# A float32 decoder trunk on one core: who subtracts the high parts of the weights

## The chip, the cores and the metric

The kernel runs on one core of a Trainium2 chip. The metric is the time of one execution on the device in microseconds (us), as the median of several runs. A profile is one execution that the hardware profiler recorded; its span runs from the first to the last instruction. The engines are named as in the profile: PE is TensorE (matrix products; PEld its loading of the stationary operand), DVE is VectorE, ACT is ScalarE, POOL is GpSimd and SP is SyncE, which issues the loads.

## The reference

Four layers act on 256 tokens of width 1024. Each layer is half an FFN, a token mixer, half an FFN, and each of the three is followed by a residual sum and a layer norm. The mixers are, by layer, DSA, FoX, MLA and DSA.

```python
for i in range(DEPTH):
    x = layer_norm(ALPHA * x + 0.5 * swiglu(x, ffn1_w13[i], ffn1_w2[i]), ln_g[i, 0], ln_b[i, 0])
    kind, j = i % N_MIXERS, i // N_MIXERS
    if kind == 0:
        y = dsa_mixer(x, dsa_w_in[j], w_out[i], cos_p, sin_p)
    elif kind == 1:
        y = fox_mixer(x, fox_w_in[j], fox_b_f[j], w_out[i])
    else:
        y = mla_mixer(x, mla_w_dqkv[j], mla_q_norm_g[j], mla_w_uq[j], mla_kv_norm_g[j],
                      mla_w_ukv[j], w_out[i], cos_m, sin_m)
    x = layer_norm(ALPHA * x + y, ln_g[i, 1], ln_b[i, 1])
    x = layer_norm(ALPHA * x + 0.5 * swiglu(x, ffn2_w13[i], ffn2_w2[i]), ln_g[i, 2], ln_b[i, 2])
```

A mixer projects x to queries, keys and values of 16 heads, forms the causal scores, the softmax and its product with the values, and multiplies by `w_out`. DSA first scores the keys with a small indexer and keeps the best of them for each query, FoX adds a bias from cumulated forget gates, and MLA projects through two low-rank latents.

## The kernel before

Each float32 product is made of three passes on TensorE. An operand is split into a high part (the value rounded to 12 significant bits) and a low part (the value less its high part), and a product is high by high plus high by low plus low by high, accumulated in PSUM (`mm3`, `mm3b`).

All weights stream through SBUF once. `unit` (line 127) takes up to 1024 columns: a load into one of six `raw` buffers, a cast to the high part on ScalarE (L144) and a subtraction for the low part (L145), both into one of 15 slots that weights and larger activations share. Two settings act on it. `self.share`, where it is not 0, cuts a unit into two pieces (`PIECES`), each with its own cast and subtraction, and gives every third unit's two subtractions to GpSimd; the other units' go to VectorE. Where it is 0, a unit is one piece and VectorE has it. `run` sets it to 3 ahead of every FFN and every mixer, and `ffn` sets it to 0 ahead of its main loop. So it acts in the mixers and, in seven of the eight FFNs, on the eight units of the first four FFN tiles (`gate` and `up`).

An FFN goes over its tiles in pairs: products of gate and up, silu, products with the second matrix. The norm at its end (`layer_norm`) adds the products to x (L232), takes the mean (L241), squares on ScalarE (L242), forms the reciprocal root on GpSimd (L218), and scales (L245, L247). Then TensorE transposes x (L202), and ScalarE and VectorE split the result into `xh` and `xl` (L190, L191 in `split`). Two token tiles of 128 follow one another through this.

In a mixer, `heads` goes over eight pairs of heads. A pair's scores are added to their bias with a row maximum (L393), the maximum is turned into a bias (L397 or L400 and L401), ScalarE takes the exponent (L403), VectorE the reciprocal (L404) and four scalings (L406). `turn` transposes the weights (L416 to L418) and splits them (`pth`, `ptl`), and `weigh` multiplies by the values. Between these steps stand products of later projections and of `w_out`, by a table that says how many. GpSimd also does the small touches of slots (L78), the zeros of the block-diagonal keys (L497, L498), the ropes (L372 to L375) and FoX's masks (L705, L706).

The order on each engine is made by the tile framework's scheduler from the order of the code and its own idea of durations. It is fixed when the program is built, and each engine executes its own in order.

Of the kernel before, what the change touches and what calls it, by code (L numbers as in the profile page):

```python
"""Hybrid decoder trunk (DSA / FoX / MLA token mixers between half-step SwiGLU FFNs) on one core.

Matrix products are float32 products on the tensor engine's one-pass float32r path: an operand is
split exactly into hi = round12(v) and lo = v - hi (12 significant bits each), and a product takes the
three passes hi*hi + hi*lo + lo*hi, accumulated in float32 in PSUM. Weights stream through SBUF once,
in units of up to 2048 columns; activations stay on chip.
"""
# [9 lines left out]
F32 = mybir.dt.float32  # L17
# [26 lines left out]
SHARE_F, SHARE_M = 3, 3  # L44
PIECES, PBUFS = 2, 1
# [6 lines left out]
class Net:  # L52
    def __init__(self, ctx, tc, a):
        self.tc, self.nc, self.a = tc, tc.nc, a
        pool = lambda name, bufs, **k: ctx.enter_context(tc.tile_pool(name=name, bufs=bufs, **k))
        self.cp = pool("const", 1)
        self.sp = pool("state", 1)
        self.kp = pool("work", 1)
        self.pp = pool("psum", 4, space=bass.MemoryType.PSUM)
        self.n = 0  # L60
        self.late, self.subs, self.share = [], 0, 0
        self.consts()

# [8 lines left out]
    def slot(self, *dims, p=P, dt=F32R, touch=True):  # L72
        """One of the 8 KB slots that weights and the larger activations share, viewed as [p, *dims].
        Slots are given in order of their first write: a touch takes one ahead of its data."""
        n = int(np.prod(dims))
        z = self.t(self.kp, [P, 2048], dt, "slot", SLOTS)[:p, :n]
        if touch:
            self.nc.gpsimd.memset(z[:, :1] if dt == F32 else z[:, :1].bitcast(F32), 0.0)  # L78
        names = "abcde"[:len(dims)]
        return z.rearrange(f"p ({' '.join(names)}) -> p {' '.join(names)}", **dict(zip(names, dims)))  # L80
# [11 lines left out]
    def consts(self):  # L92
        """What the first products need; the rest comes in late_consts."""
        nc, a = self.nc, self.a
        self.mhalf = self.const("mhalf", [P, 1])
        nc.vector.memset(self.mhalf, -0.5)
        self.ident = self.const("ident", [P, P])
        nc.sync.dma_start(self.ident, a["c_ident"])
        self.x = [self.t(self.sp, [P, D], F32, f"x{t}", 1) for t in range(NT)]
        self.load_x(0)  # L100
        # the activation table and the tensor engine's clock are brought up while the loads run
        z = self.tok()
        nc.gpsimd.memset(z, 0.0)
        nc.scalar.activation(z[:, :1], z[:, :1], AF.Silu)
        ps = self.ps("b")
        for i in range(WARM):
            nc.tensor.matmul(ps[:, :P], z[:, P:2 * P], z[:, 2 * P:3 * P], start=True, stop=True)
# [19 lines left out]
    def unit(self, src):  # L127
        """Loads and splits a DRAM view [128, a, b], up to 1024 columns at a time; gives (hi, lo) [128, b]
        of each of a."""
        nc = self.nc  # L130
        _, a, b = src.shape
        out = []
        step = -(-a // -(-a // (1024 // b)))
        for i in range(0, a, step):
            n = min(step, a - i)
            raw = self.w([P, 1024], "raw", RAWS)[:, :n * b]
            z = self.slot(2, n * b, touch=False)
            h, l = z[:, 0], z[:, 1]
            nc.sync.dma_start(raw.rearrange("p (a b) -> p a b", a=n), src[:, i:i + n])
            self.subs += 1  # L140
            e = nc.gpsimd if self.share and self.subs % self.share == 0 else nc.vector
            m = n * b // (PIECES if self.share else 1)
            for c in [slice(o, o + m) for o in range(0, n * b, m)]:
                nc.scalar.copy(h[:, c], raw[:, c])  # L144
                e.tensor_sub(l[:, c], raw[:, c], h[:, c].bitcast(F32))  # L145
            out += [(h[:, j * b:(j + 1) * b], l[:, j * b:(j + 1) * b]) for j in range(n)]
        return out

    def rows(self, w, k0, k1, c0, c1):
        """Rows k0*128.. of a [K, N] matrix as [128, k, cols]."""  # L150
        return w[k0 * P:k1 * P, c0:c1].rearrange("(k p) c -> p k c", p=P)

    def cols(self, w, c0, n):
        """Columns c0..c0+n of a [1024, N] matrix: (hi, lo) of each K tile."""
        return self.unit(self.rows(w, 0, KT, c0, c0 + n))
# [13 lines left out]
    def flush(self):  # L169
        """Emits the transposes of x that wait for a place among other products."""  # L170
        for z in self.late:
            z()
        self.late = []

    def proj(self, us, t, out, flush=None):
        """out[tokens of tile t, n] = x @ w over the K tiles of us."""
        q = slice(t * P, (t + 1) * P)
        for k, (h, l) in enumerate(us):
            if k == flush:
                self.flush()  # L180
            self.mm3(out, self.xh[:, k, q], self.xl[:, k, q], h, l, k == 0, k == len(us) - 1)

    def projb(self, us, i, out, k0=0):
        """out[columns i*128.. of w, tokens] = (x @ w) transposed; us are the K tiles from k0."""
# [36 lines left out]
    def layer_norm(self, t, acc, mult, eps, last=False):  # L221
        """x <- LN(mult * x + acc); scaling the argument by two and eps by four changes nothing."""
        nc = self.nc
# [30 lines left out]
    def begin_out(self, w, n, src, tag):  # L254
        """A [256 n, 1024] matrix by units of two K tiles; src(i) gives (hi, lo) [128, tokens] of K tile i."""
        self.ow, self.on, self.osrc = w, n, src
        self.ou, self.acc, self.otag = {}, {}, tag

    def out_mm(self, k, t, halves=(0, 1)):
        """Adds unit k's product for token tile t."""  # L260
# [13 lines left out]
    def out_end(self, t, ks):  # L274
        """The last units of a token tile, the first half of the columns done early."""
# [7 lines left out]
    def ffn(self, w13, w2, ln, first=False, last=False):  # L283
# [4 lines left out]
        if not first:  # L288
            # the first four ff tiles by token tile, tokens on partitions
# [25 lines left out]
        self.share = 0  # L315
        for j in range(pairs):
# [5 lines left out]
            # a bank to each column tile where the K tiles come in two parts  # L322
# [43 lines left out]
    def rope(self, z, tab, t, half):  # L366
        """Turns z [128, heads, 2*half] in place; tab [128, tile, (cos cos | sin sin), 2*half]."""
# [9 lines left out]
    def softmax(self, scores, bias, scale, cq=None):  # L377
        """One pair of heads: scores(t) gives PSUM [128 queries, 2, keys]. The products are emitted; the rest is
        left as a function that gives the weights by t and head."""
# [3 lines left out]
        def rest():  # L383
# [14 lines left out]
            else:  # L398
                # the row's own cum enters the logits and the maximum alike
# [11 lines left out]
    def turn(self, views):  # L411
        """The weights of a pair transposed: [128 keys, (head, query)] of key tile 0 and 1."""
# [12 lines left out]
    def weigh(self, ph, pl, v, i, oh, ol):  # L425
        """O transposed of a pair; columns i*128.. of v are its values, oh and ol [128, tokens]."""
# [12 lines left out]
    def heads(self, project, weights, w_out, plan, done=0, begun={}, more=()):  # L439
        """The eight pairs of heads, two to a group. project(g) yields between chunks of its work and then  # L440
        has group g ready; weights(p) gives the softmax of pair p and (v, column block) of its values.
        Between the steps of a pair stand chunks of later groups' projections (plan: how many after a pair's
        softmax and after its transposes) and products of w_out."""
# [41 lines left out]
    def values(self, w, c0, v):  # L485
        """V of two pairs from columns c0.. of w."""
# [7 lines left out]
    def new_kz(self, n=2):  # L494
        """Block diagonal K of pairs: a head's rows are zero in the other head's columns."""
# [10 lines left out]
    def pair_scores(self, qh, ql, kh, kl):  # L506
        """qh, ql [128 (2 heads), 256 tokens]; kh, kl [128, 2, 256] block diagonal."""
# [10 lines left out]
    def dsa(self, w_in, w_out, ln):  # L518
# [51 lines left out]
        def select(t):  # L570
            """Additive mask of the keys that are causal and among the top ones."""
# [60 lines left out]
    def fox(self, w_in, b_f, w_out, ln):  # L632
        nc = self.nc
        scale = HD ** -0.5
        # forget gates: heads on partitions
# [22 lines left out]
        # log sigmoid(z) = min(z, 0) - log(1 + exp(-|z|))  # L658
# [6 lines left out]
        # every query's row of key terms, by a broadcast through memory  # L665
# [32 lines left out]
        def weights(p):  # L698
            g, i = p // 2, p % 2
            q, kz, ck = ready[g]  # L700
            # mask the diagonal blocks of this pair's key terms
# [131 lines left out]
    def run(self):  # L833
# [4 lines left out]
        for i in range(DEPTH):  # L838
            j = i // 3
            self.share = SHARE_F  # L840
            self.ffn(a["ffn1_w13"][i], a["ffn1_w2"][i], (i, 0), first=i == 0)
            self.share = SHARE_M
# [7 lines left out]
            self.share = SHARE_F  # L850
# [13 lines left out]
def _shape_constants():  # L864
    """Identity, causal mask and rotary tables: they depend on the shapes alone."""
# [34 lines left out]
```

## Time and profile before

| what | value |
|---|---|
| median of 3 runs | 2077.57 us (2077.02 to 2078.26) |
| span of the profiled execution | 2077.2 us |
| PE busy | 2021.1 us (97%) |
| DVE busy | 1271.0 us (61%) |
| ACT busy | 1030.3 us (50%) |
| POOL busy | 320.7 us (15%) |
| chain that ended last | PE 82%, DVE 12%, ACT 3% |

The profiled execution is known by its span alone; the median of the runs is 0.4 us above it. A busy share is a mean over stages: the FFNs take most of the span and the four mixers lie between them, at 197 to 352 us (DSA), 729 to 862 (FoX), 1239 to 1351 (MLA) and 1726 to 1878 (DSA). In rows of the timeline the number in brackets at the end is the idle time of the engine before the row and what ended it.

### The profile page before, as it was taken

The numbers are of one execution on the slowest core, as the hardware profiler recorded it, in microseconds if no ns is written. First come the engines' busy times: TensorE is split into PE (matmuls) and PEld (weight loads), VectorE is DVE, ScalarE is ACT, GpSimd is POOL, SyncE is SP. The second block draws the span as 40 slices with busy tenths as digits, with TensorE's granted clock in tenths as the row PEclk, the third lists the DMA queues.
The fourth block names the chain that finished last, engine by engine and source line by source line (L and its number), as shares of the span: only waits on it lengthen the run. The fifth ranks groups of instructions, "written<-read, shape, count | busy, mean of one in ns | idle before, by whom it ended". The sixth has DMA issues, their size and how long they took to land.

```text
span 2077.2 us, 34193 instructions
## 1 busy us (share of the span) xinstructions
PE 2021.1 (97%) x13430; PEld 1853.2 (89%) x13430; DVE 1271.0 (61%) x2069; ACT 1030.3 (50%) x1714; POOL 320.7 (15%) x454
## 2 busy tenths in 40 slices
PE   9999998999999998999999999899999999989998
PEld 8999986999899987799989998689989999978997
DVE  6455889544644469855465456964465546887453
ACT  5443476444444357644444436754444444675441
POOL 0002542000100145200110014400020005430000
PEclk9999999999999999999999999999999999999999
DMA  9754534665656454565665543566656564347550
GB/s 304 226 184 138 153 122 155 214 188 176 212 183 188 150 162 155 185 208 184 183 203 182 186 121 105 180 214 185 187 178 208 187 180 131 119 125 237 189 184 21
DMA packets 253025, 362.98 MB, mean 175 GB/s; under 512 B 11856, under 2 KB 204128, under 8 KB 252864
## 3 DMA queue, kind: packets, MB, share of 16 engines
q1 hardware_dynamic: 252080, 358.30, 54.7%
q0 software_dynamic: 784, 2.51, 0.4%
q8 instruction: 105, 1.72, 0.3%
q14 instruction: 56, 0.46, 0.1%
HBM read 359.69 MB, written 1.06 MB: 174 GB/s over the span
## 4 chain that ended last, share of the span: by engine, by line
PE 82%; DVE 12%; ACT 3%; issue 2%; POOL 0%; DMA 0%; SPq 0%; DVEq 0%; ACTq 0%; POOLq 0%
PE psa L166 14%; PE psa L167 14%; PE psa L165 14%; PE psb L159 8%; PE psb L160 8%; PE psb L161 8%; PE psa L159 5%; PE psa L161 5%; PE psa L160 5%; DVE slot L145 3%; DVE slot L191 2%; DVE s L406 2%; ACT s L403 1%; PE psb L202 1%; ACT slot L144 1%
## 5 line engine op out<-in xcount | busy, mean ns | idle before, releaser
L145 DVE TENSOR_TENSOR slot<-raw,slot 128x1024 fp32r<-128x1024 f32 (+4 forms) x724 | 773.1, 1089 | 617.5 <-ACT slot L144 614.9
L144 ACT CAST slot<-raw 128x1024 fp32r<-128x1024 f32 (+5 forms) x854 | 693.8, 849 | 652.0 <-issue 354.9
L166 PE MATMUL psa<-xh,slot 128*128 128x256 f32 x2496 | 707.6, 284 | 3.8 <-DVE slot L145 3.8
L165 PE MATMUL psa<-xh,slot 128*128 128x256 f32 x2496 | 707.4, 284 | 0.0
L167 PE MATMUL psa<-xl,slot 128*128 128x256 f32 x2496 | 707.1, 283 | 0.0
L166 PEld LDWEIGHTS psa<-xh,slot 128*128 128x128 f32 x2496 | 479.7, 192 | 7.6 <-DVE slot L145 4.6
L165 PEld LDWEIGHTS psa<-xh,slot 128*128 128x128 f32 x2496 | 479.6, 192 | 3.0
L167 PEld LDWEIGHTS psa<-xl,slot 128*128 128x128 f32 x2496 | 479.6, 192 | 0.0
L159 PE MATMUL psb<-slot,slot 128*128 128x512 f32 (+2 forms) x800 | 308.1, 385 | 9.0 <-DVE slot L191 4.8
L160 PE MATMUL psb<-slot,slot 128*128 128x512 f32 (+2 forms) x800 | 306.9, 384 | 1.9 <-DVE slot L191 1.9
L161 PE MATMUL psb<-slot,slot 128*128 128x512 f32 (+2 forms) x800 | 305.3, 382 | 1.2 <-DVE slot L191 1.2
L159 PE MATMUL psa<-slot,xh 128*128 128x256 f32 (+5 forms) x736 | 241.1, 328 | 0.0
L160 PE MATMUL psa<-slot,xh 128*128 128x256 f32 (+5 forms) x736 | 238.6, 324 | 0.0
L161 PE MATMUL psa<-slot,xl 128*128 128x256 f32 (+5 forms) x736 | 238.1, 324 | 0.0
L145 POOL TENSOR_TENSOR slot<-raw,slot 128x512 fp32r<-128x512 f32 (+4 forms) x130 | 183.5, 1428 | 306.1 <-ACT slot L144 297.1
L159 PEld LDWEIGHTS psb<-slot,slot 128*128 128x128 f32 (+1 forms) x800 | 150.9, 189 | 37.7 <-ACT slot L190 5.3
L78 POOL MEMSET slot<- 128x1 f32 (+1 forms) x88 | 8.5, 101 | 1118.4 <-PE psb L161 972.1
L161 PEld LDWEIGHTS psb<-slot,slot 128*128 128x128 f32 (+1 forms) x800 | 150.9, 189 | 30.9 <-DVE slot L191 1.5
L160 PEld LDWEIGHTS psb<-slot,slot 128*128 128x128 f32 (+1 forms) x800 | 151.2, 189 | 28.3 <-DVE slot L191 2.7
L159 PEld LDWEIGHTS psa<-slot,xh 128*128 128x128 f32 x736 | 140.6, 191 | 10.3 <-ACT xh L190 0.3
L160 PEld LDWEIGHTS psa<-slot,xh 128*128 128x128 f32 x736 | 140.6, 191 | 10.2
L161 PEld LDWEIGHTS psa<-slot,xl 128*128 128x128 f32 x736 | 140.4, 191 | 10.4
(150 smaller groups left out, 1696.7 us busy)
## 6 DMA issues: line engine op xcount, KB each, us to landing
raw<-in_ffn_w SPq DMA_DIRECT2D x528, 512.0 KB, 4.2
raw<-in_dsa_w_in SPq DMA_DIRECT2D x48, 512.0 KB, 3.8
raw<-in_w_out SPq DMA_DIRECT2D x32, 512.0 KB, 3.6
raw<-in_fox_w_in SPq DMA_DIRECT2D x24, 512.0 KB, 3.8
ln_g<-in_ln_g SPq DMA_DIRECT2D x12, 512.0 KB, 5.5
ln_b<-in_ln_b SPq DMA_DIRECT2D x12, 512.0 KB, 5.8
slot<-scratch_cum POOLq DMA_DIRECT2D x4, 512.0 KB, 5.4
raw<-in_mla_w_ukv SPq DMA_DIRECT2D x4, 512.0 KB, 3.9
```

Source lines behind the costliest of these rows:

```text
L144: nc.scalar.copy(h[:, c], raw[:, c])
L145: e.tensor_sub(l[:, c], raw[:, c], h[:, c].bitcast(F32))
L159: mm(out, sh, mh, start=start, stop=False)
L160: mm(out, sh, ml, start=False, stop=False)
L161: mm(out, sl, mh, start=False, stop=stop)
L165: mm(out, sh, mh, start=start, stop=False)
L166: mm(out, sl, mh, start=False, stop=False)
L167: mm(out, sh, ml, start=False, stop=stop)
L191: self.nc.vector.tensor_sub(lo, src, hi.bitcast(F32))
L202: self.nc.tensor.transpose(ps[:, i * P:(i + 1) * P], self.x[t][:, k * P:(k + 1) * P], self.ident)
L403: nc.scalar.activation(sv, sv, AF.Exp, bias=nb[:, c:c + 1], scale=scale, accum_out=l[:, c:c + 1])
L406: nc.vector.tensor_scalar(sv, sv, l[:, c:c + 1], None, op0=ALU.mult)
```

## The change

`self.share` and its count are gone; `self.pieces` says into how many pieces a unit is cut, and VectorE has all subtractions. `run` sets it to 2 ahead of an FFN, `ffn` to 1 ahead of its main loop, and nothing sets it ahead of a mixer. So the eight first units of an FFN are still cut in two, and a mixer's units are one piece each.

```diff
-SHARE_F, SHARE_M = 3, 3
...
-        self.late, self.subs, self.share = [], 0, 0
+        self.late, self.pieces = [], 1
...
-            self.subs += 1
-            e = nc.gpsimd if self.share and self.subs % self.share == 0 else nc.vector
-            m = n * b // (PIECES if self.share else 1)
+            m = n * b // self.pieces
             for c in [slice(o, o + m) for o in range(0, n * b, m)]:
                 nc.scalar.copy(h[:, c], raw[:, c])
-                e.tensor_sub(l[:, c], raw[:, c], h[:, c].bitcast(F32))
+                nc.vector.tensor_sub(l[:, c], raw[:, c], h[:, c].bitcast(F32))
...
         pairs = (NFF - f0) // 2
-        self.share = 0
+        self.pieces = 1
...
-            self.share = SHARE_F
+            self.pieces = PIECES
             self.ffn(a["ffn1_w13"][i], a["ffn1_w2"][i], (i, 0), first=i == 0)
-            self.share = SHARE_M
...
-            self.share = SHARE_F
+            self.pieces = PIECES
             self.ffn(a["ffn2_w13"][i], a["ffn2_w2"][i], (i, 2), last=i == DEPTH - 1)
```

Of the subtractions of weights, the program before has 472 of 1024 columns, 210 of 512 and 42 of other widths on VectorE and 118 of 512 and 12 of other widths on GpSimd. The changed program has 580 of 1024, 112 of 512 and 27 of other widths (384 to 960) on VectorE. The scheduler's order changes with it. The changed program's line numbers are 1 to 4 lower than those above (L142 is L145, L188 is L191, L199 is L202, L229 is L232, L242 is L245, L244 is L247, L394 is L397, L403 is L406). In names of buffers the last number is a running one; the first says which buffer.

First place: VectorE where the first FFN ends and the first DSA begins. `x0_1_71` and `x1_2_72` are x of token tiles 0 and 1, `psb_53` and `psb_54` the two halves of tile 1's last products. Before:

```order
L245 SCALAR_TENSOR_TENSOR x0_1_71<-x0_1_71,lnst_191_1842,ln_g_97_979 128x512 x2
L247 SCALAR_TENSOR_TENSOR x0_1_71<-x0_1_71,rstd_196_1852,ln_b_98_980 128x512 x2
L232 SCALAR_TENSOR_TENSOR x1_2_72,lnst_199_1908<-x1_2_72,psb_53_526 128x512
L191 TENSOR_TENSOR xl_190_1841<-psb_197_1882,xh_189_1840 128x4x128
L191 TENSOR_TENSOR xl_190_1841<-psb_198_1889,xh_189_1840 128x4x128
L145 TENSOR_TENSOR slot_230_2045<-raw_229_2044,slot_230_2045 128x512 x2
L145 TENSOR_TENSOR slot_232_2052<-raw_231_2051,slot_232_2052 128x512
L232 SCALAR_TENSOR_TENSOR x1_2_72,lnst_199_1908<-x1_2_72,psb_54_527 128x512
```

And now:

```order
L242 SCALAR_TENSOR_TENSOR x0_1_71<-x0_1_71,lnst_191_1842,ln_g_97_979 128x512 x2
L229 SCALAR_TENSOR_TENSOR x1_2_72,lnst_199_1908<-x1_2_72,psb_53_526 128x512
L229 SCALAR_TENSOR_TENSOR x1_2_72,lnst_199_1908<-x1_2_72,psb_54_527 128x512
L238 TENSOR_SCALAR lnst_199_1908<-lnst_199_1908 128x1
L244 SCALAR_TENSOR_TENSOR x0_1_71<-x0_1_71,rstd_196_1852,ln_b_98_980 128x512 x2
L213 TENSOR_SCALAR ve_203_1916<-lnst_199_1908 128x1
L242 SCALAR_TENSOR_TENSOR x1_2_72<-x1_2_72,lnst_199_1908,ln_g_97_979 128x512 x2
L188 TENSOR_TENSOR xl_190_1841<-psb_197_1882,xh_189_1840 128x4x128
L188 TENSOR_TENSOR xl_190_1841<-psb_198_1889,xh_189_1840 128x4x128
```

The last step of tile 0's norm moved behind both sums of tile 1, and the low part of x behind the first scalings of tile 1.

Second place: TensorE there. Before:

```order
L161 MATMUL psb_53_526<-slot_188_1818,slot_165_1649 128x512
L202 MATMUL psb_197_1882<-c_ident_69,x0_1_71 128x128 x4
L202 MATMUL psb_198_1889<-c_ident_69,x0_1_71 128x128 x4
L159 MATMUL psb_54_527<-slot_182_1797,slot_134_1333 128x512
L160 MATMUL psb_54_527<-slot_182_1797,slot_134_1333 128x512
```

And now:

```order
L158 MATMUL psb_54_527<-slot_188_1818,slot_165_1649 128x512
L199 MATMUL psb_197_1882<-c_ident_69,x0_1_71 128x128 x4
L199 MATMUL psb_198_1889<-c_ident_69,x0_1_71 128x128 x4
L156 MATMUL psa_222_1965<-slot_206_1925,xh_189_1840 128x320
L157 MATMUL psa_222_1965<-slot_206_1925,xh_189_1840 128x320
L156 MATMUL psa_223_1966<-slot_212_1940,xh_189_1840 128x264
L157 MATMUL psa_223_1966<-slot_212_1940,xh_189_1840 128x264
L156 MATMUL psa_239_2057<-slot_230_2033,xh_189_1840 128x256
L158 MATMUL psa_222_1965<-slot_206_1925,xl_190_1841 128x320
```

The transposes moved behind all twelve products of `psb_54`, and five products with `xh` stand between them and the first that needs `xl`. Where FoX ends they moved behind twelve products in the same way, at each DSA's end behind six; at the other seams they stand where they stood.

Third place: VectorE in the first DSA, from the maximum of a pair to the scalings of the pair before. Before:

```order
L145 TENSOR_TENSOR slot_393_3153<-raw_392_3152,slot_393_3153 128x512
L397 TENSOR_SCALAR nb_357_2888<-m_355_2886 128x4
L404 RECIPROCAL l_346_2847<-l_346_2847 128x4
L406 TENSOR_SCALAR s_344_2845<-s_344_2845,l_346_2847 128x128 x2
L406 TENSOR_SCALAR s_344_2845<-s_344_2845,l_346_2847 128x256 x2
```

And now:

```order
L142 TENSOR_TENSOR slot_393_3105<-raw_392_3104,slot_393_3105 128x1024
L394 TENSOR_SCALAR nb_357_2844<-m_355_2842 128x4
L401 RECIPROCAL l_346_2803<-l_346_2803 128x4
L403 TENSOR_SCALAR s_344_2801<-s_344_2801,l_346_2803 128x128 x2
L403 TENSOR_SCALAR s_344_2801<-s_344_2801,l_346_2803 128x256 x2
```

A whole unit stands where half of one stood.

## Rows read from the trace of the kernel before

**Rows 1.** Windows: stretch, us, busy (x) of PE, PEld, DVE, ACT, POOL; PEclk; sum
```profile
211.00:352.00 141.00, 128.70 (x899) 117.78 (x898) 120.65 (x314) 90.40 (x230) 60.10 (x79) 0.99 0.43 135
...
741.00:862.00 121.00, 111.19 (x709) 97.25 (x707) 96.27 (x236) 78.52 (x191) 56.84 (x56) 0.97 0.49 155
...
1263.00:1351.00 88.00, 80.09 (x463) 65.69 (x461) 76.47 (x213) 69.90 (x188) 38.77 (x65) 1.00 0.44 142
...
1741.00:1878.00 137.00, 126.48 (x887) 116.20 (x886) 115.09 (x310) 89.52 (x229) 58.92 (x79) 0.99 0.44 133
...
sum 2077.20, PE 2021.11 PEld 1853.23 DVE 1271.05 ACT 1030.31 POOL 320.73; mean PE 87.87 PEld 80.58 DVE 55.26 ACT 44.80 POOL 13.94
```

**Rows 2.** Groups by line and form: xcount, busy us, mean ns, idle before
```profile
L145 DVE TENSOR_TENSOR slot<-raw,slot 128x1024 fp32r<-128x1024 f32 (+4 forms) x724 | 773.1, 1089 | 617.5 <-ACT slot L144 614.9
...
L145 DVE TENSOR_TENSOR slot<-raw,slot 128x1024 fp32r<-128x1024 f32 x472 | 569.4, 1223 | 551.8 <-ACT slot L144 549.9
L145 DVE TENSOR_TENSOR slot<-raw,slot 128x512 fp32r<-128x512 f32 x210 | 177.8, 876 | 41.4 <-ACT slot L144 40.6
...
L406 DVE TENSOR_SCALAR s<-s,l 128x256 f32<-128x256 f32 x64 | 29.7, 505 | 0.0
...
L406 DVE TENSOR_SCALAR s<-s,l 128x128 f32<-128x128 f32 x64 | 20.8, 367 | 0.8
...
L145 POOL TENSOR_TENSOR slot<-raw,slot 128x512 fp32r<-128x512 f32 x118 | 170.8, 1464 | 187.4 <-ACT slot L144 178.4 <-issue 8.7 <-POOL slot L498 0.2
```

**Rows 3.** Timeline of DVE and POOL, 302 to 306 us: start, us
```profile
302.70 1.01 DVE L406 TENSOR_SCALAR s<-s,l 128x128 f32<-128x128 f32 x4
303.62 0.69 DVE L145 TENSOR_TENSOR slot<-raw,slot 128x512 fp32r<-128x512 f32 x1
304.56 3.15 DVE L145 TENSOR_TENSOR slot<-raw,slot 128x512 fp32r<-128x512 f32 x2 [0.25 <-ACT slot L144]
...
303.56 3.60 POOL L145 TENSOR_TENSOR slot<-raw,slot 128x512 fp32r<-128x512 f32 x2 [5.42 <-ACT slot L144]
```

**Rows 4.** Timeline of DVE and PE at two stalls of PE
```profile
335.18 3.48 DVE L145 TENSOR_TENSOR slot<-raw,slot 128x512 fp32r<-128x512 f32 x2
...
339.43 0.51 PE L167 MATMUL psb<-ptl,slot 128*128 128x512 f32 x1 [2.01 <-DVE ptl L191]
...
1312.53 3.10 DVE L406 TENSOR_SCALAR s<-s,l 128x128 f32<-128x128 f32 x4
...
1315.43 0.33 PE L417 MATMUL psb<-c_ident,s 128*128 128x128 f32 x1 [1.70 <-DVE s L406]
```

**Rows 5.** Waits of PE: us in total, times, longest us
```profile
PE psb L202 <- DVE x L247: 5.9, 7, 1.6
...
PE psb L417 <- DVE s L406: 4.3, 5, 1.7
PE psb L165 <- DVE ptl L191: 3.8, 5, 1.6
PE psa L166 <- DVE slot L145: 3.8, 4, 2.0
...
PE psb L167 <- DVE ptl L191: 3.6, 5, 2.0
```

**Rows 6.** Windows at lowered clock (columns as in rows 1)
```profile
267.20:270.60 3.40, 3.40 (x14) 3.11 (x14) 2.81 (x19) 1.99 (x3) 1.39 (x4) 0.50 0.71 233
827.00:833.80 6.80, 4.88 (x14) 3.92 (x15) 6.11 (x16) 3.48 (x12) 2.24 (x2) 0.50 0.73 230
```

**Rows 7.** Timeline of DVE and ACT at two norms
```profile
192.09 1.15 ACT L242 ACTIVATE s<-x,lnst 128x1024 f32<-128x1024 f32 x1 [7.77 <-DVE lnst L241]
...
194.76 1.41 DVE L247 SCALAR_TENSOR_TENSOR x<-x,rstd,ln_b 128x512 f32<-128x512 f32 x2
196.55 0.69 DVE L232 SCALAR_TENSOR_TENSOR x<-x,psb 128x512 f32<-128x512 f32 x1 [0.39 <-PE psb L161]
...
537.46 3.46 DVE L247 SCALAR_TENSOR_TENSOR x<-x,rstd,ln_b 128x512 f32<-128x512 f32 x2
```

## The prediction

> **What bounds the kernel now.** I read first the windows by stage [rows 1]. Over the span of 2077.20 us TensorE is busy for 2021.11, so only 56 us can be won without taking products away. The rows of the four mixers (DSA, FoX, MLA, DSA) hold most of them: 141.00 less 128.70, 121.00 less 111.19, 88.00 less 80.09 and 137.00 less 126.48, together 40.5 us idle. VectorE is busy there for 80 to 87 percent of the time and GpSimd for over two fifths, so the question is what these two do to each other.
>
> Then I read the groups by form [rows 2]. VectorE's subtraction of 1024 columns takes 1223 ns. That of 512 columns takes 876 on the mean, far more than half. GpSimd's 118 of 512 columns take 1464 ns each.
>
> The timeline shows why [rows 3]. At 303.56 GpSimd starts two halves, which take 3.60 us. VectorE's two that start at 304.56 beside them take 3.15 us, though the one just before took 0.69. From 303.56 to 307.71 the two engines did five halves in 4.15 us; VectorE alone would do five in 3.45. **So GpSimd's help is worth nothing while VectorE subtracts beside it.** The slowing is not limited to the subtractions: four scalings of the softmax (L406) take 1.01 us at 302.70 and 3.10 at 1312.53 [rows 3, 4].
>
> Last I read what TensorE waits for. Right behind such places [rows 4]: VectorE's two halves at 335.18 take 3.48 us instead of 1.4, and TensorE then waits 2.01 us for the L191 behind them; the slow scalings at 1312.53 are followed by a wait of 1.70. In total [rows 5]: 5.9 us at the transposes of x for L247, 4.3 at those of the softmax weights for L406, 3.8 and 3.6 in the value products for L191, 3.8 in FoX's projections for the weights' low parts.
>
> **The change, part by part.**
>
> *Removed from GpSimd:* all 130 subtractions (118 of the common form, [rows 2]). What GpSimd keeps (touches, ropes, block-diagonal zeros, the powers of the norms) no longer stands behind them. Off the path as such.
>
> *VectorE's load.* Before, 724 subtractions of mean 1089 ns [rows 2], 788 us, of which 472 x 1.223 = 577 are the FFNs' whole units, which stay. So 211 us go. In the changed order there are 108 more whole units (132 us at 1.223), 112 halves of the FFNs' first units (77 us at 0.69) and 27 of odd widths with 19,328 columns in all (24 us at 0.157 plus 1.04 ns a column, the line through 512 and 1024). That is 234 us, 23 more, although VectorE takes over a third. The L406 give back: 29.7 + 20.8 us busy for 32 times four [rows 2], against 32 x 1.01 = 32 us, 18 less. Other slowed forms add to that, such as L247, whose pair takes 3.46 us at 537.46 and 1.41 at 194.76 [rows 7]. So VectorE's load stays about where it is.
>
> [...]
>
> *ScalarE.* By the two orders 328 casts of 512 columns become 112, and 472 of 1024 become 580. ScalarE is busy for 1030 of the 2077 us [rows 1], so I count nothing; if that cover were gone, it would be a gain, since one whole takes the place of two.
>
> *Stalls that go.* Of [rows 5] I take off 3 us of the 5.9 for L247 (the norm's own length stays), 4 of the 4.3 for L406, 5 of the 7.4 for L191 in the value products, 1.5 of the 3.8 in FoX: 13.5. These groups hold 21.4 us in all. Of the other 19 or more in the mixers I take 8, because the same slowing lies earlier in those chains; the rest are dependences that stay, as index scores and the last norm. Bounds: 5 us, if the slowing was mostly in slack, and 34, if nearly all goes. I take 21.5, between them, by the rows that stand right behind a slowed instruction.
>
> *Clock.* [...] I take 4, between 0 and 5.1.
>
> *What the new order costs.* The order is fixed by a scheduler and it moved at the seams. Where the first FFN ends, the norm of token tile 0 had been finished beside the products of tile 1, and the transposes stood ahead of twelve of these. Now L247 of tile 0 stands on VectorE behind both L232 of tile 1, and the transposes behind all twelve. Nothing covers the norm there. From the last product on: L232 0.69, the first L247 0.7 [rows 7], and with the small L241 and the hand-overs between them an estimated 0.4, that is 1.8 us. Four transposes take about 0.4; the second L247 is 0.3 later than they are. The low part of x then stands behind two L245 that wait for ScalarE's square of tile 1 (1.15 us [rows 7], from 1.0 after the last product), so it is there after 4.7 us, when TensorE has had 0.7 us of products and 0.9 of transposes. Loss: 3.2 us, where there was none. At the end of FoX the transposes move behind twelve products too, but VectorE keeps L247 ahead of the last L232: 1.1 more. At the two DSA ends they move by six products: nothing, six being left as cover. Sum 4.3, between 2 (if the first products stretch over it) and 8 (a clock drop behind it).
>
> *Whole units instead of halves.* Softmax steps that were behind a half of 0.69 are now behind a whole of 1.22, and TensorE's first product of a unit waits half a unit longer. Most are prefetched. Sixty-four softmax passes (two to each of 32 pairs); if every fifth meets one on the path, 13 x 0.53 = 7 us. Bounds 0 and 17 (every second one). I take 6.5.
>
> *Sum.* 21.5 + 4 - 4.3 - 6.5 = 14.7 us less. The profiled execution has a span of 2077.2; the median of the runs shown is 2077.57, 0.4 above the span. **Forecast: 2063 us.**
>
> **The rivals.**
>
> *All of it (2045).* If VectorE's lateness is behind nearly all idle time, 34 us of stalls and 5 of the clock go, and seams and wholes cost 7 together: 32 less. For it: VectorE, directly or through what it feeds, ends most of the waits. Against it: the wholes are longer and some waits are dependences.
>
> *No change (2077).* The slowing goes, but the longer pieces take its place on the path: 21.5 + 4 of gains against 8 at the seams and 17 for the wholes. For it: VectorE's own sum hardly falls. Against it: the waits of [rows 4] sit at slowed instructions.
>
> *Slower (2086).* One mechanism: whole units in front of L397 and L406. As the third place of the order shows for one pass, a whole stands where a half stood; if every second pass meets one on the path (17 us), the seams cost 4.3, and only half the gain is real, since the stalls move to the next wait (12.8), the kernel is 8.5 us slower. With half the gain it decides from 16 passes: 16 x 0.53 + 4.3 = 12.8. Against it: a slowed half was at times longer than a whole is, 1.7 us each at 335.18. [...]
>
> *That the change does not do what it says* can be excluded: no subtraction of the weights is left on GpSimd in the changed order. It does more than its words: the FFNs' first units move as well, and the mixers' units are no longer cut in halves.
>
> **How the numbers follow.** Forecast 0.60, all of it 0.17, no change 0.11, slower 0.12. A measurement of this kernel tells 0.2 percent, 4 us, from no change. The forecast's own range is 2052 to 2072, all of it faster. Faster: 0.60 + 0.17 and a little of the third, 0.78; same 0.10; slower 0.12. The range leaves out the lower half of the second case and nearly all of the last: 2046 to 2078.
>
> **What would show it.** In the profile after: no L145 on GpSimd; VectorE's 512 wide subtractions at 0.69 us with no spread up to 2.1; L406 near 1.0 for four; VectorE's busy time within 15 us of 1271; TensorE idle in the mixers down from 40.5 to about 22; a new wait of 2 to 4 us at the first L202 behind the first FFN. It is wrong if idle time in the mixers stays above 35 with VectorE at its own pace: then the wholes took the place of the slowing. It is wrong the other way if the seam shows no wait and idle falls below 15.

## The result, and the profile after

The changed kernel takes 2046.59 us (median of 4 runs, 2044.67 to 2049.12) against 2077.3 of the kernel before on the same chip: a ratio of 0.9851 with an interval of 0.9837 to 0.9865, so 30.7 us less. The forecast was 14.7 us less. The time lies just inside the range, at its lower edge; the direction was right, and the gain is twice what was forecast. The profiled execution has a span of 2047.4 us.

The page's line of busy times:

```profile
PE 2017.6 (99%) x13430; PEld 1855.6 (91%) x13430; DVE 1261.7 (62%) x2064; ACT 1017.9 (50%) x1579; POOL 140.1 (7%) x324
```

GpSimd's busy time fell from 321 to 140 us [rows 1]. VectorE now does all subtractions and is busy for 9 us less than before. Why shows in the groups by form (count, busy us, mean ns):

```profile
L142 DVE TENSOR_TENSOR slot<-raw,slot 128x1024 fp32r<-128x1024 f32 x580 | 699.7, 1222 | 574.0 <-ACT slot L141 570.3
L142 DVE TENSOR_TENSOR slot<-raw,slot 128x512 fp32r<-128x512 f32 x112 | 72.5, 684 | 24.0 <-ACT slot L141 23.7
L244 DVE SCALAR_TENSOR_TENSOR x<-x,rstd,ln_b 128x512 f32<-128x512 f32 x48 | 34.0, 748 | 0.9 <-POOL rstd L215 0.9
L403 DVE TENSOR_SCALAR s<-s,l 128x256 f32<-128x256 f32 x64 | 20.2, 358 | 0.0
L403 DVE TENSOR_SCALAR s<-s,l 128x128 f32<-128x128 f32 x64 | 16.2, 294 | 0.5
```

The 512 columns went from 876 to 684 ns, the scalings of the softmax from 505 and 367 to 358 and 294 [rows 2]. The windows of the four mixers, in the form of [rows 1] and moved with the work:

```profile
211.00:346.00 135.00, 134.84 (x957) 124.31 (x956) 116.76 (x315) 91.84 (x208) 27.48 (x60) 1.00 0.48 147
735.00:847.00 112.00, 106.08 (x690) 94.66 (x688) 93.42 (x230) 76.61 (x164) 23.41 (x34) 0.97 0.52 162
1255.00:1331.00 76.00, 69.78 (x412) 58.98 (x411) 67.61 (x201) 60.88 (x157) 11.77 (x33) 1.00 0.40 125
1721.00:1850.00 129.00, 128.86 (x918) 118.89 (x917) 113.29 (x308) 88.22 (x203) 26.65 (x58) 1.00 0.49 150
```

TensorE's idle time in them is 0.16, 5.92, 6.22 and 0.14 us: 12.4 where there were 40.5. The second and third end ahead of waits at the seam behind them; by the stages of the table below it is 15.3 where it was 41.1. In the two DSAs hardly any idle time is left. What TensorE still waits for (total us, times, longest):

```profile
PE psb L199 <- DVE x L244: 6.2, 3, 3.7
PE psb L413 <- DVE s L403: 4.5, 1, 4.5
PE psa L156 <- ACT xh L187: 3.2, 3, 2.1
```

Of the waits of [rows 5], that for L145 is gone and those of the value products for L191 are down from 7.4 to 1.1 us. The three above stand at the seams (the ends of the first FFN, of FoX and of MLA) and in FoX. The timeline at the end of the first FFN and at the end of MLA (the start, us, and in brackets the idle time before and who ended it):

```profile
200.09 1.32 PE L199 MATMUL psb<-c_ident,x 128*128 128x128 f32 x8 [1.70 <-DVE x L244]
...
1330.19 1.52 PE L199 MATMUL psb<-c_ident,x 128*128 128x128 f32 x8 [3.68 <-DVE x L244]
...
1333.78 0.80 PE L156 MATMUL psa<-slot,xh 128*128 128x512 f32 x1 [2.07 <-ACT xh L187]
```

At the end of MLA TensorE had waited before too, for a shorter time:

```profile
1350.44 1.29 PE L202 MATMUL psb<-c_ident,x 128*128 128x128 f32 x8 [1.63 <-DVE x L247]
```

At each of the two seams and in FoX TensorE's granted clock was 0.50 for 6.8 us, half clock in what follows (the column behind GpSimd's):

```profile
201.30:208.10 6.80, 6.09 (x24) 5.98 (x24) 6.80 (x10) 4.09 (x6) 2.56 (x4) 0.50 0.49 163
771.30:778.10 6.80, 4.24 (x19) 4.05 (x20) 6.53 (x19) 6.73 (x20) 1.85 (x3) 0.50 0.01 4
1331.10:1337.90 6.80, 4.73 (x14) 3.46 (x13) 6.28 (x12) 4.48 (x7) 0.99 (x1) 0.50 0.55 161
```

That is 20.4 us at half clock after the start of the program, where there were 13.6 before, of which 10.2 stand in [rows 6]. Products of 256 columns start 0.213 us apart in such a stretch (from 775.79 to 777.92) and 0.120 at a clock of 1.00 (from 768.01 to 769.09); those of 512 columns 0.43 (from 1334.37 to 1337.79) and 0.23 (from 1338.09 to 1339.93). So 44 to 46 percent of such a time is lost.

To see which stage gained, I measure each stage from the end of the last transposes of x (L202, after L199) of one norm to that of the next, by their times in the timeline. The last two columns are runs of the section below.

| stage, us | before | after | halves | one unit |
|---|---|---|---|---|
| first FFN | 200.6 | 206.8 | 206.4 | 200.4 |
| first DSA | 151.9 | 137.2 | 137.0 | 137.0 |
| FFNs behind it (2) | 377.9 | 376.4 | 376.4 | 376.4 |
| FoX | 132.9 | 128.1 | 125.3 | 126.0 |
| FFNs (2) | 377.0 | 376.9 | 376.1 | 376.1 |
| MLA | 109.6 | 109.8 | 102.7 | 102.3 |
| FFNs (2) | 379.8 | 379.0 | 381.6 | 381.6 |
| second DSA | 149.5 | 137.1 | 137.0 | 137.1 |
| last FFN, to its last product | 178.2 | 178.2 | 178.2 | 178.2 |

The DSAs gave 27.1 us, FoX 4.8, MLA nothing, and the first FFN took 6.2 back. Of the 29.8 us between the two spans 1.9 lie ahead of the first row and behind the last.

### The profile page after: what moved, and what is told of

Read it like the earlier page. It is cut to its first block, busy times and chain, and to the rows that moved or that the text cites. A ratio compares the mean times of both kernels' runs of the same rounds, so it can differ in the third digit from the quotient of the medians.

```text
span 2047.4 us, 33890 instructions
## 1 busy us (share of the span) xinstructions
PE 2017.6 (99%) x13430; PEld 1855.6 (91%) x13430; DVE 1261.7 (62%) x2064; ACT 1017.9 (50%) x1579; POOL 140.1 (7%) x324
## 4 chain that ended last, share of the span: by engine, by line
PE 92%; DVE 3%; ACT 2%; DMA 2%; issue 1%; POOL 0%; SPq 0%; DVEq 0%; ACTq 0%; POOLq 0%
PE psa L163 14%; PE psa L164 14%; PE psa L162 14%; PE psb L156 8%; PE psb L157 8%; PE psb L158 8%; PE psa L156 7%; PE psa L157 7%; PE psa L158 7%; DMA raw<-in_ffn_w 1%; PE psb L199 1%; ACT slot L141 1%; ACT s L400 1%; DVE slot L142 1%; PE psb L162 0%
## 5 line engine op out<-in xcount | busy, mean ns | idle before, releaser
L142 DVE TENSOR_TENSOR slot<-raw,slot 128x1024 fp32r<-128x1024 f32 (+4 forms) x719 | 795.5, 1126 | 622.7 <-ACT slot L141 618.8
L141 ACT CAST slot<-raw 128x1024 fp32r<-128x1024 f32 (+4 forms) x719 | 680.6, 972 | 671.0 <-issue 344.3
L157 PEld LDWEIGHTS psa<-slot,xh 128*128 128x128 f32 x736 | 141.4, 192 | 10.2
L187 ACT CAST slot<-psb 64x256 fp32r<-64x256 f32 (+4 forms) x158 | 63.4, 411 | 39.4 <-DVE slot L188 25.9
```

Source lines behind the costliest of these rows:

```text
L142: nc.vector.tensor_sub(l[:, c], raw[:, c], h[:, c].bitcast(F32))
L157: mm(out, sh, ml, start=False, stop=False)
L187: self.nc.scalar.copy(hi, src)
```

## Experiments

Theory H (hindrance): GpSimd's subtractions hold up VectorE, and TensorE's waits follow. Its rivals: the gain comes from fewer, larger pieces (W), or from GpSimd's own results having come late.

**Unread subtractions.** The changed kernel, with GpSimd's work put back as work that nobody waits for:

```diff
...
+            if self.idle and self.subs % 3 == 0:
+                m = n * b // 2
+                for o in (0, m):
+                    y = h[:, o:o + m].bitcast(F32)
+                    u = self.w([P, 512], "unread", 1)[:, :m]
+                    nc.gpsimd.tensor_sub(u, y, y)
...
```

`self.idle` is set for the FFNs' first units and the mixers' units, those that GpSimd had a third of.

> The changed kernel, in which GpSimd also subtracts, for every third unit of the mixers and of the FFNs' first products, the high part from itself in two halves into a scratch tile that nobody reads: added work, the results are unchanged. VectorE and ScalarE do all that they do in the changed kernel and nobody waits for GpSimd's result. Theory H: VectorE's instructions stretch to 2 us and more beside it, TensorE waits again as before, and most of the 30 us are given back, 2068 to 2085. Theory W or lateness: nothing that is read comes later, so it stays at 2047, at most 5 away.

Measured: 2077.21 us, ratio to before 1.0004 (0.9994 to 1.0014). All of the gain is given back, with VectorE's and ScalarE's work that of the changed kernel. The busy times and groups by form of this run (here L144 is L142, L196 is L188, L411 is L403):

```profile
PE 2023.9 (97%) x13430; PEld 1857.1 (89%) x13430; DVE 1313.7 (63%) x2064; ACT 1018.9 (49%) x1579; POOL 328.9 (16%) x454
...
L144 DVE TENSOR_TENSOR slot<-raw,slot 128x512 fp32r<-128x512 f32 x112 | 91.3, 851 | 18.0 <-ACT slot L143 17.4
L196 DVE TENSOR_TENSOR ptl<-psb,pth 128x512 fp32r<-128x512 f32 x32 | 22.0, 688 | 3.6 <-ACT pth L195 3.0
L411 DVE TENSOR_SCALAR s<-s,l 128x256 f32<-128x256 f32 x64 | 23.9, 414 | 0.0
L150 POOL TENSOR_TENSOR unread<-slot 128x512 f32<-128x512 f32 x118 | 168.6, 1429 | 182.0 <-ACT slot L143 177.6
```

VectorE's busy time rose from 1261.7 to 1313.7 us: 52 us for 130 added instructions, 0.40 each. An unread half takes 1.04 us where nothing holds it and the halves of the kernel before 1.30, so the added work is no heavier than what was removed. The first DSA went from 137.2 to 146.7 us and the second from 137.1 to 151.5. The four mixers together are 30.7 us longer than in the changed kernel, and in each of them TensorE, VectorE and ScalarE execute the same sequence of instructions as there (by operation, name and shape, buffer numbers left out): there the scheduler's order is no part of the difference. The order did change at the end of the first FFN, which took 200.2 us, 6.6 less, so the total is net of that. TensorE's waits in the DSAs are back too, the splits of q and k (L196) among them:

```profile
PE psb L164 <- DVE slot L196: 4.4, 4, 2.5
```

W is out, since the mixers' pieces are whole here, and so is lateness of GpSimd's subtractions, which nobody reads. Its ropes and zeros still stand behind them, and TensorE's waits for GpSimd rose from 2.5 to 6.2 us in all; those for VectorE rose from 13.5 to 28.9. VectorE's subtractions out of PSUM (`ptl`, L196) kept their 688 ns, the 512 columns of L144 with both inputs in SBUF did not (851 where they took 684). Nine of the 32 `ptl` ran beside an unread subtraction, in 0.68 to 0.69 us; one of them, between two GpSimd pieces that keep their time as well:

```profile
1310.01 2.16 POOL L150 TENSOR_TENSOR unread<-slot 128x512 f32<-128x512 f32 x2 [2.75 <-ACT slot L143]
```

```profile
1310.79 0.68 DVE L196 TENSOR_TENSOR ptl<-psb,pth 128x512 fp32r<-128x512 f32 x1
```

Of the 112 subtractions of 512 columns (L144), the 41 that ran beside one took 1.15 us on the mean and the others 0.68.

**Unread copies.** The same, with `nc.gpsimd.tensor_copy(u, y)`.

> As the run with unread subtractions (which took 2077.2 us and gave all of the gain back), but GpSimd's added 130 pieces are copies, with one input, of the same columns into the same unread tile; results are unchanged. Theory P (VectorE is held only where both engines have two inputs or so to read from SBUF, that is, the second input is what hinders): about 2047, at most 5 away, and VectorE's 512 wide subtractions near 0.69 us. Theory Q (any large GpSimd instruction on SBUF holds VectorE for its length): 2062 to 2080, with 512 wide subtractions spread up to 2 us as with the subtractions.

Measured: 2054.71 us, ratio 0.9889 (0.9873 to 0.9906), between the two theories. The groups by form:

```profile
L144 DVE TENSOR_TENSOR slot<-raw,slot 128x512 fp32r<-128x512 f32 x112 | 80.5, 754 | 21.1 <-ACT slot L143 20.8
L150 POOL COPY unread<-slot 128x512 f32<-128x512 f32 x118 | 119.6, 1014 | 188.1 <-ACT slot L143 184.9
```

VectorE's busy time is 1280.4 us, 18.7 more than after, 0.14 for each copy. Copies hold VectorE too, for a third as long as subtractions (0.40 each), and a quarter of the gain is given back (8.1 of 30.6 us). The copies are shorter, by 30 percent on the mean and by 40 where nothing holds them (0.61 us beside 1.04), so length alone does not explain it; what else does stays open.

**Whole units, GpSimd keeps its third.** The kernel before with `PIECES, PBUFS = 1, 1`.

> The kernel before with whole units in place of halves, GpSimd keeping every third: the merging without the removal. Theory H: GpSimd's pieces of 1024 columns take near 2.6 us and hold VectorE for as long, so no gain: 2075 to 2095. Theory W: a good part of the gain shows, 2055 to 2065. A third (lateness: TensorE waits because GpSimd's own low parts are finished late) would make it slower than before too, by more, 2085 and up, with waits of TensorE for GpSimd's subtractions in the list of waits.

Measured: 2081.63 us, ratio 1.0028 (1.0016 to 1.0040). The groups by form, with 59 of GpSimd's wholes:

```profile
L145 DVE TENSOR_TENSOR slot<-raw,slot 128x1024 fp32r<-128x1024 f32 x577 | 724.9, 1270 | 604.8 <-ACT slot L144 602.7
L145 POOL TENSOR_TENSOR slot<-raw,slot 128x1024 fp32r<-128x1024 f32 x59 | 151.5, 2568 | 181.2 <-ACT slot L144 176.9 <-issue 3.7 <-POOL slot L498 0.6
```

Merging alone gains nothing, which speaks against W. The longest waits of TensorE are again for VectorE, not for GpSimd's subtractions.

**Halves, all on VectorE.** The changed kernel with the mixers' units cut as before:

```diff
+            self.pieces = PIECES
             if i % 3 == 0:
                 self.dsa(a["dsa_w_in"][j], a["w_out"][i], (i, 1))
```

> All subtractions stay on VectorE as in the changed kernel, but the mixers' units are cut in halves again, as before the change: the removal from GpSimd without the merging. Theory H (hindrance: GpSimd's two-input subtractions hold up whatever VectorE does in SBUF, and TensorE's waits follow from that): 2047 us, at most 5 away from the changed kernel's 2046.6, VectorE's 512 wide subtractions near 0.69 us with no spread. Theory W (the gain comes in good part from fewer and larger casts and subtractions on ScalarE and VectorE): 2055 to 2065, and TensorE's idle time in the mixers up by 8 us or more. The prediction's own term for whole units (6.5 us lost by them) would have halves faster: 2040.

Measured: 2041.94 us, ratio 0.9835 (0.9820 to 0.9850). The removal alone carries the whole gain and 4.7 us by the medians beyond it, though the intervals of this kernel and the changed one overlap (the profiled executions differ by 7.0). By the stages both DSAs are the same within 0.3 us. The difference is in FoX (2.8) and at the end of MLA (7.1, less 2.7 in the FFN behind it), where the halves leave products beside the norm of tile 0. Its square on ScalarE and its transposes on TensorE:

```profile
1322.23 1.15 ACT L239 ACTIVATE s<-x,lnst 128x1024 f32<-128x1024 f32 x1
```

```profile
1326.19 1.29 PE L199 MATMUL psb<-c_ident,x 128*128 128x128 f32 x8
```

There is no wait in front of the transposes, where the changed kernel has 3.68. The last product ends 0.1 us after the start of these transposes. In the changed kernel the square starts only 0.1 us behind the last product's end (1326.5):

```profile
1326.64 1.14 ACT L239 ACTIVATE s<-x,lnst 128x1024 f32<-128x1024 f32 x1
```

**GpSimd's third in the mixers alone.** The kernel before, with `self.share = 10**9` in place of `SHARE_F` at both FFNs.

> The kernel before, GpSimd taking its third in the mixers alone; the FFNs' first units are split by VectorE in halves. Theory H with all of its effect in the mixers: 2070 to 2077, as before. If the FFNs' first units and the seams between stages hold a good part of the gain, 2055 to 2065.

Measured: 2062.81 us, ratio 0.9938 (0.9923 to 0.9953). So the mixers' own units cost 20.9 us (2062.81 less 2041.94), net of the 5.9 that the seam of the first FFN loses with them (200.5 to 206.4), and those of the FFNs' first products 13.8 or so (2076.64, the kernel before measured beside it, less 2062.81). The latter are split ahead, while a mixer still runs: without GpSimd there the first DSA fell from 151.9 to 146.6 us.

**One unit back on GpSimd.** The run with halves, in which the first unit of the first DSA goes to GpSimd:

```diff
...
+            self.subs += 1
+            e = nc.gpsimd if self.subs in self.gp else nc.vector
...
+            self.subs, self.gp = 0, (1,) if i == 0 else ()
...
```

> The run with halves (2041.9 us), in which GpSimd takes back one single unit, the first of the first DSA, in two halves: by the order of the instructions the transposes of token tile 0 behind the first FFN then stand ahead of twelve products again, as before the change. Seam theory: the changed kernel and the run with halves lose 6 us there (the stretch of the first FFN took 206.8 and 206.4 us where it took 200.6 before: a stall of 2.4 and half the clock for 6.8 us); it goes back to 200 to 201, in all 2036, between 2033 and 2038. Rival: the loss there has another cause (start-up, transfers): that stretch stays above 204 and the time at 2042.

Measured: 2035.79 us, ratio 0.9794 (0.9780 to 0.9808), the lowest median of all and clear of the changed kernel's interval. The busy times, and the window that was at half clock:

```profile
PE 2009.5 (99%) x13430; PEld 1850.3 (91%) x13430; DVE 1270.5 (62%) x2197; ACT 1030.8 (51%) x1714; POOL 141.7 (7%) x326
...
201.00:208.00 7.00, 7.00 (x57) 7.00 (x56) 6.13 (x12) 2.98 (x7) 5.13 (x10) 1.00 0.96 295
```

TensorE is busy throughout at a clock of 1.00, and the stage takes 200.4 us, where the run with halves takes 206.4. The seam costs 6 us, about half of it by the clock behind the wait (an estimate: 45 percent of 6.8 us, by the pace shown above, is 3.1).

**FoX's masks.** In the changed kernel one stall is left in FoX. The timeline of VectorE and GpSimd in front of it:

```profile
765.25 5.33 DVE L397 SCALAR_TENSOR_TENSOR nb<-m,cq 128x4 f32<-128x4 f32 x1
```

```profile
765.67 2.82 POOL L703 TENSOR_TENSOR slot<-slot,c_diag 128x256 f32<-128x256 f32 x4
768.46 0.73 POOL L702 TENSOR_TENSOR slot<-slot,c_diag 128x256 f32<-128x256 f32 x1
769.16 1.39 POOL L703 TENSOR_TENSOR slot<-slot,c_diag 128x256 f32<-128x256 f32 x2
```

An instruction on four columns takes 5.33 us and ends when seven additions of GpSimd are through. I moved these sixteen additions to VectorE, in the changed kernel and in the one with halves (`nc.gpsimd.tensor_add` to `nc.vector.tensor_add`, two lines).

> The changed kernel with the sixteen additions of FoX's masks on VectorE instead of GpSimd. Theory H: the changed kernel's one long stall left in FoX (4.5 us at 769, behind a 128x4 instruction of VectorE that took 5.33 us beside seven of these additions) goes, and with it the half clock behind it (6.8 us at half, 3.4 lost): 2039, between 2037 and 2043. Rival: the sixteen additions (0.3 to 0.5 us each on VectorE) stand in front of the softmax instead, and the stall stays: 2045 to 2050.

> Halves in the mixers, all subtractions on VectorE (2041.9 us), and FoX's masks on VectorE too. Theory H: the stall of 4.2 us at 770 goes and 3.4 us of half clock with it: 2034, between 2032 and 2038. If the two edits mend the same thing, no faster than the better of them alone, 2039 to 2042.

Measured: 2046.91 us, ratio 0.9854 (0.9837 to 0.9871), no gain (FoX took 128.7 us, in the changed kernel 128.1); and with halves 2039.25, ratio 0.9820 (0.9804 to 0.9836), not told apart from halves alone. Both expectations of H fall. VectorE and TensorE in the first of them:

```profile
760.27 0.42 DVE L702 TENSOR_TENSOR slot<-slot,c_diag 128x256 f32<-128x256 f32 x1 [6.06 <-DMA slot<-scratch_cum]
```

```profile
763.49 0.39 PE L158 MATMUL psb<-slot,slot 128*128 128x256 f32 x1 [3.71 <-DVE slot L188]
```

The masks wait for the key terms to come back through memory, and on VectorE that wait stands in front of a split of q (L188, at 762.74) that TensorE needs. On GpSimd no split stood behind it.

**Half of the masks.** The run with one unit, and `p < 4` on GpSimd, the rest on VectorE.

> As the run with one unit on GpSimd, and FoX's masks of pairs 4 to 7 on VectorE, those of pairs 0 to 3 left on GpSimd: GpSimd's row of seven additions back to back, beside which one small instruction of VectorE took 5.3 us, becomes shorter, and VectorE's own masks stand behind the split of q, so that its wait for their transfer holds up nothing that TensorE needs. Theory H: the stall of 4.2 us in FoX shrinks to 2 or less, 2 to 6 us faster than the run with one unit (more where the half clock behind it goes too). Rival: VectorE's masks wait for the transfer in front of the first scores, as when all sixteen moved: same time as the run with one unit, within 2 us.

Measured: 2037.78 us, ratio 0.9801 (0.9788 to 0.9815), the rival's outcome. VectorE waits 5.02 us for a transfer of the key terms (L706 here is L703 above), and TensorE 4.80 in front of the first scores:

```profile
759.61 2.59 DVE L706 TENSOR_TENSOR slot<-slot,c_diag 128x256 f32<-128x256 f32 x2 [5.02 <-DMA slot<-scratch_cum]
```

The transfer is not all of it: VectorE's two additions then took 2.59 us beside GpSimd's, where one took 0.42 above. A stall of 3.4 to 4.8 us at this place survives every arrangement tried. An earlier start of the transfer was not tried.

**Rotations on VectorE too.** The run with halves and masks, and `e = self.nc.vector` in `rope`.

> As the run with halves and masks, and the rotations (four instructions of two inputs each, 96 in all of some width) move from GpSimd to VectorE as well, so that GpSimd keeps next to nothing with two inputs but the powers of the norms. Theory H: the waits of TensorE for the rotations (1.7 us in MLA) go and VectorE has room, 2 us faster than the run with halves and masks at most, within 0.2 percent of it. Rival: VectorE's own queue becomes the bound in the mixers where rotations stand before scores, 3 to 8 us slower than that run.

Measured: 2047.88 us, ratio 0.9858 (0.9843 to 0.9874), 8.6 us slower than the run it starts from, a little more than the rival's 3 to 8. Its list of waits begins with

```profile
PE psb L413 <- DVE s L403: 4.8, 3, 2.1
```

which that run does not have. The rival's direction holds, though 2.4 of the 8.6 us lie in the first FFN, ahead of all rotations, whose end is at half clock for 6.8 us in place of 3.4 (from 200 to 345 us the mean clock is 0.98 in place of 0.99): small work that GpSimd does off the path is better left there.

## Why the prediction was half right

- **VectorE's load**, forecast within 15 us of 1271: 1261.7. Right, with both marks of the mechanism (512 columns at 684 ns, four scalings at 1.14 us on the mean, where they took 1.58). That GpSimd's help is worth nothing beside VectorE was the right reading of [rows 3], and the unread subtractions show it as the cause. By their lengths without such company the third on GpSimd would have been help: in the run with whole units the five GpSimd pieces that had no VectorE instruction with all its inputs in SBUF beside them took 2.40 us, against 1.22 for one on VectorE, so that three units would be done in 2.4 us by both engines and in 3.7 by VectorE alone (an estimate). The runs decide against it: 2081.63 us with whole units and that third, 2046.59 in the changed kernel.
- **Stalls that go**, 21.5 with bounds of 5 and 34: this is the step that failed. The run with one unit is the clean measure, since it keeps the seam of the first FFN. Its TensorE idle time is 2034.1 less 2009.5, 24.6 us, against 56.1 before: 31.5 us gone, near the upper bound, 28.7 of them in the four mixers by their stages (41.1 to 12.4), in a span shorter by 43.1. Wrong was that of the other 19 us in the mixers 8 go and "the rest are dependences that stay". In the DSAs all went. The waits for splits and scores that I had counted as dependences went with GpSimd's subtractions and came back with the unread ones. I had credited only waits with a slowed row in plain sight, and the two shown in [rows 4] were the visible part.
- **Clock**, forecast 4 us of gain: half-clock time rose by 6.8 us instead, a loss of 3.1 by the pace shown above. The forecast's 4, with its bound of 5.1, takes half of the 10.2 us of [rows 6] as lost; that half no run shows, the pace gives 4.6. The old drops of [rows 6] did not stay where they were; but new ones stand behind the first FFN, in FoX and behind MLA. In the run with one unit, without the seams, only 3.4 us at half clock are left between start and end: 10.2 less than before, 4.6 us gained. That is near the upper bound, though the bound left out 3.4 us at half clock in the second DSA (from 1796.4). So the term was right for the stalls and belonged, with the other sign, to the seams as well.
- **Seams**, 4.3 with bounds of 2 and 8. The first FFN's, forecast at 3.2, has waits of 1.70 and 0.71 and, with the clock, 6.2 us; the text named "a clock drop behind it" only for the bound. FoX's is 0.81 and 0.46 where a wait of 0.83 stood before, 0.4 more (forecast 1.1 more), the DSAs' nothing (as forecast). MLA's was missed, 3.68 and 2.07 us where it was 1.63. The transposes stand behind the last product in both kernels, as the text before the prediction says, and I had looked no further. But the square of tile 0 started 1.9 us ahead of the end of that product before (1346.88) and 0.1 behind it now (1326.64). With the clock behind it, it is why MLA gained nothing.
- **Whole units**, 6.5 us of loss by softmax passes that meet a whole: in the DSAs, where half of the passes are, halves and wholes differ by 0.4 us together. That the size comes near (4.7 us by the medians) is luck: it comes by another way, the order at MLA's end and whatever holds FoX 2.8 us longer. As a price of passes it fell.
- **The sum**, by the spans: 29.8 us less, 15.1 beyond the forecast. Of these 10.0 are the stalls and 0.6 the clock, both by the run with one unit. Another 7.0 are TensorE's own busy time, which the prediction put at nothing: it fell by 11.6 us in that run, of which the clock's 4.6 are one part. Of the 7.0, 1.5 are the clock at the program's start (6.8 us at half before and in the run with halves, 3.4 there and in the changed kernel), and 5.5 stay open. Against them, what the changed kernel loses to that run, the seams and whole units with their clock, is 13.3 where 10.8 stood.
- **The rivals.** "All of it" gave 2045, within 1.6 us of the measured time. Of its parts the stalls were of the right size; its clock term had the wrong sign, and its 7 us for seams and wholes were about what those cost without the clock. "Slower" named whole units in front of L397 and L406; the one wait of that kind in the list (L403, 4.5 us) stands behind FoX's masks, not behind a whole.

## What to carry to other kernels

Where VectorE is late, look first at what GpSimd does in SBUF at the same moment: instructions of one form with a mean far above their shortest are the sign (here 876 ns where they take 684 without GpSimd's subtractions), and unread work on GpSimd is the test. If slowed instructions stand in a chain, credit all idle time of that stage as a candidate, not only the waits that have a slowed row in front. Then read every seam in the new order: taking work from one engine moved the scheduler's order at several of them, it cost most at two, and one unit put back mended that of the first FFN.

## What was not expected of the hardware

The hold goes both ways. In the run with unread subtractions GpSimd's two pieces took 4.53 us, though at 325.12 one such piece took 1.04, while VectorE's wholes beside them kept their pace (2.35 for two):

```profile
302.87 4.53 POOL L150 TENSOR_TENSOR unread<-slot 128x512 f32<-128x512 f32 x2 [5.88 <-ACT slot L143]
...
325.12 1.04 POOL L150 TENSOR_TENSOR unread<-slot 128x512 f32<-128x512 f32 x1 [12.20 <-ACT slot L143]
```

```profile
303.02 2.35 DVE L144 TENSOR_TENSOR slot<-raw,slot 128x1024 fp32r<-128x1024 f32 x2
```

In FoX it is VectorE that stands, 5.33 us on four columns, beside seven additions of GpSimd. On which instructions of VectorE are held, the runs show that subtractions out of PSUM kept their time (688 ns in both), and that those with both inputs in SBUF did not (851 beside 684); the scalings L411, with one input in SBUF, were held too (414 beside 358). At these two places the one that stands has the earlier start in the profile: GpSimd's first piece starts at 302.87, 0.15 us ahead of VectorE's wholes, and its two pieces take 2.45 us more than two of 1.04, about the 2.35 of both wholes; VectorE's instruction at 765.25 starts 0.42 us ahead of GpSimd's additions and stands for all seven. What decides which of the two stands no run shows. It stood for two and for seven instructions of the other in a row.
